# A two-layer hybrid encoder on one core: TensorE's order taken from a scheduler, or written out with delays in ticks

## The chip, the core and the metric

One core of a Trainium2 chip runs the whole program. The core has TensorE (PE, matrix products into PSUM), VectorE (DVE), ScalarE (ACT), GpSimd (POOL) and SyncE (SP), which issues most of the DMAs. The metric is the device time of one execution in microseconds (us); smaller is better. The median of three runs before the change is 1895.78 us (1894.39 to 1896.45).

## The reference

Sequence 512, model width 1024, two layers. Each layer normalizes x, projects it to 7168 columns, and mixes tokens in three ways: differential attention (4 heads, two softmaxes each over all 512 keys), a convolution module (gated linear unit, 31-tap depthwise convolution, layer norm, SiLU) and neighbourhood attention (8 heads, an 8 x 16 window on an 8 x 64 grid, with a bias). Sigmoid gates merge them. An FFN and a gated per-layer input ("ple") follow, and a last norm ends the program.

```python
for i in range(DEPTH):
    h = rmsnorm(x, norm_mix[i])
    qa, ka, va, glu_in, qc, kc, vc, gates = jnp.split(h @ w_in[i], SPLITS, axis=-1)
    ya = diff_attention(qa, ka, va, ...)
    yb = conformer_conv(glu_in, ...)
    yc = neighbourhood_attention(qc, kc, vc, rpb[i])
    ga, gb, gc = jnp.split(jax.nn.sigmoid(gates), 3, axis=-1)
    merged = ga * (ya @ w_br_a[i]) + gb * (yb @ w_br_b[i]) + gc * (yc @ w_br_c[i])
    x = x + merged @ w_o[i]
    h = rmsnorm(x, norm_ffn[i])
    x = x + (jax.nn.silu(h @ w_ffn_gate[i]) * (h @ w_ffn_up[i])) @ w_ffn_down[i]
    h = rmsnorm(x, norm_ple[i])
    x = x + jax.nn.sigmoid(h @ w_ple_gate[i]) * (p[i] @ w_ple_in[i])
return rmsnorm(x, norm_final)
```

## The kernel before

**Layout and products.** Activations lie transposed: a chunk is 128 model columns by 512 tokens, and h is 8 such chunks. Every operand is split into a high part (rounded to the format that PE multiplies) and a low part, the remainder; `mm3` (L116) makes three products for one: high x high, high x low, low x high. `gemm` (L122) sums up to eight chunks of rows into one PSUM tile of 128 x 512, 24 products of 512 columns. `weights` (L105) loads one block of 128 x 1024 with a DMA on SP's queue and splits it on ACT (high, L82) and DVE (low, L96), with a priority 400 instructions ahead of its place; there are two raw buffers and three split ones. PSUM has four tiles for projections (`mm`), two for scores (`sc`), one for transposes (`tr`) and one for value products (`av`).

**Who sets the order.** A scheduler orders each engine's instructions when the program is traced: among the ready ones it takes the earliest by program order, with weights moved ahead, going by a model of the durations. On the chip each engine then runs its own list in order. PE's order is set in this way too, so projections that come later in the program are put where attention waits.

**Norms.** The scale 1/rms is not applied to h but to each projection when it leaves PSUM (`self.rb`, one value per token, spread over partitions). `rows_rstd` (L136) makes it: four transposes of the sum of squares (L142), a reduce (L144) and a scalar step (L146) on DVE, the power -0.5 on POOL (L148), four transposes that spread it (L151). The instructions that need it come behind it in the program.

**One layer** (`layer`, L263): `glu` (8 projections), then four pairs of neighbourhood heads (`natten_in`, `natten_out`) and four heads of differential attention (`diff_in`, `diff_out`), each with its query and key projections, value products for every second one (`values`, L382, 256 columns wide), then `gate_c`, `branch_c`, `merge_a`, `gate_b`, `merge_b`, `w_o`, `ffn`, `ple`. `stack` (L566) brings queries and keys into their final place with four DMAs for a query and eight for a key on SP's queue; `rope` adds four more. A neighbourhood pair makes four units (two halves of the tokens, two heads): scores (L591), bias and softmax on DVE, ACT and POOL, transposes by PE (L476 to L481), a split out of PSUM, value products (L498 to L501). A head of differential attention does the same with two softmaxes (`probs`, L657; transposes L633, value products L639), and ends with a norm of its own over 128 columns.

**Convolution.** `taps` (L324) yields the 124 tap instructions of a layer, each on DVE over 128 x 512. `background` (L339) puts some of them behind given evictions, by the tuple `BG`: 4 behind each neighbourhood eviction, 2 behind each rope, 4 in gate C, 1 in branch C, 3 and 1 in merge A. `conv` (L351), called between merge A and gate B (AT = 8), sums the four tiles, has PE make the mean (L361), and normalizes.

**Start and end.** `build` loads the eight chunks of x in turn, with the first weight block in four pieces and the second whole, and PE starts on two blocks. `final` (L761) sums the squares, makes the power, transposes the result and stores it in eight DMAs of 256 KB.

Of the kernel before, what the change touches and what calls it, by code (L numbers as in the profile page):

```python
# [47 lines left out]
TUNE = {}  # L48
AT = 8
LOOK = 0  # L50
NORM = (1, 1)
START = (0, 1)
BG = (4, 2, 4, 1, 3, 4, 1, 4)
GAP = 464
# [7 lines left out]
class Net:  # L62
    def __init__(self, nc, tc, a):
        self.nc, self.tc, self.a = nc, tc, a
        self.uid = 0
        self.phase = "pre"
        self.act_set = None
        self.act_now = []
        self.act_prev = []

# [34 lines left out]
    def weights(self, ap, n, ahead=None, parts=1):  # L105
        with self.tc.high_priority(offset=self.w_ahead if ahead is None else ahead):
            raw = self.sb("wr", [P, 1024])
            hi = self.sb("wh", [P, 1024], F32R)
            lo = self.sb("wl", [P, 1024], F32R)
            for c in range(parts):  # L110
                s = slice(c * n // parts, (c + 1) * n // parts)
                self.nc.sync.dma_start(raw[:, s], ap[:, s])
                self.split(hi[:, s], lo[:, s], raw[:, s])
        return hi, lo
# [7 lines left out]
    def gemm(self, out, ap, acts, first=True, last=True):  # L122

        n = len(acts)
        for o in range(0, n, 8):
            c = min(8, n - o)
            wh, wl = (self.first.pop(0) if self.first
                  else self.weights(ap[:, o * P:(o + c) * P], c * P))
            for k in range(c):
                s = slice(k * P, (k + 1) * P)  # L130
                h = acts[o + k]
                h = h if isinstance(h, tuple) else (h[:, 0, :], h[:, 1, :])
                self.mm3(out, wh[:, s], wl[:, s], h[0], h[1],
                         first and o + k == 0, last and o + k == n - 1)

    def rows_rstd(self, sq, n):  # L136


        nc = self.nc
        st = self.ps("tr", (P, 4, P))  # L140
# [7 lines left out]
        nc.gpsimd.tensor_tensor(col, ms, self.power, ALU.pow)  # L148
        bc = self.ps("tr", (P, 4, P))
        for c in range(4):  # L150
            nc.tensor.transpose(bc[:, c, :], col[:, c:c + 1].to_broadcast([P, P]), self.ident)  # L151
        return col, bc.rearrange("p a b -> p (a b)")
# [6 lines left out]
    def norm_chunk(self, k, x, g, tag, st):  # L159
# [4 lines left out]
        self.sumsq(k, x, st)  # L164
# [11 lines left out]
    def build(self):  # L176
        nc, tc, a = self.nc, self.tc, self.a
        self.w_ahead = 400
        self.bufs = dict(wr=2, wh=3, wl=3, h=8, qk=4, kh=2, v=4, pt=2, y=5, z=5, x=8, t=8, rp=4,
                         e=4, a=3, r=4, ss=1, sm=8, rc=4, b=3, s=4)  # L180
        self.pbufs = dict(mm=4, sc=2, tr=1, av=1)
        tune = dict(TUNE)
        BG, AT, NORM, START, LOOK = (tune.pop(k, globals()[k]) for k in ("BG", "AT", "NORM", "START", "LOOK"))
        self.bg, self.at, self.norm, self.start, self.look = BG, AT, NORM, START, LOOK
        self.w_ahead = tune.pop("w_ahead", self.w_ahead)
        for t, n in tune.items():
            (self.pbufs if t in self.pbufs else self.bufs)[t] = n
        with tc.tile_pool(name="sb", bufs=1) as self.pool, \
# [3 lines left out]
            xsrc = a["xT"]  # L192
            h, st = [], []
            self.first = []
            self.parts = self.sb("par", [P, PAR], bufs=1)
            self.small()
            nc.sync.dma_start(self.parts, a["par"])
            self.consts()
            for k in range(KD):
                x = self.sb("x", [P, 512])  # L200
                nc.sync.dma_start(x, xsrc[k])
                h.append(self.norm_chunk(k, x, self.par(0, "mix", k), "h", st))
                if k in self.start:
                    m = len(self.first)
                    col0 = OFF_GLU + (CB if m % 2 == 0 else 0) + m // 2 * P
                    self.first.append(self.weights(a["w_in"][0, col0 // P], 1024, 0,
                                                   4 if m == 0 else 1))
            col, bc = self.rows_rstd(st[0], D)
            for i in range(L):
                h, col, bc = self.layer(i, h, col, bc, xsrc, xs)  # L210
                xsrc = xs
# [51 lines left out]
    def layer(self, i, h, col, bc, xsrc, xs):  # L263
        self.i, self.h = i, h
        self.col, self.rb = col, self.spread(bc)
# [5 lines left out]
        yc, ya, st, sd = [], [], {}, {}  # L271
        work = [(self.natten_in, self.natten_out, n, yc, st) for n in range(HC // 2)]
        work += [(self.diff_in, self.diff_out, n, ya, sd) for n in range(HA)]
        ready = []
        for n in range(len(work) + self.look):
            if n < len(work):
                w = work[n]
                ready.append(w[0](w[2], w[4]))
            if n >= self.look:
                w = work[n - self.look]  # L280
                w[1](w[2], w[3], *ready[n - self.look])
        acc = self.gate_c()
        self.branch_c(acc, yc)
        yb = []
        then = lambda m: yb.extend(self.conv(cs)) if m == self.at else None
        self.merge_a(ya, acc, then)
        gb = self.gate_b(then)
        then(2 * KD)
        mg = self.merge_b(yb, acc, gb)
        x, h, bc = self.w_o(mg, xsrc)  # L290
        self.rb = self.spread(bc)
        pairs = self.inputs()
        h, col, bc = self.ffn(h, x)
        self.rb = self.spread(bc)
        return self.ple(h, x, xs, pairs)

    def proj(self, col0):
        ps = self.ps("mm")
# [3 lines left out]
    def glu(self, zs):  # L302
        self.phase = "glu"
        nc = self.nc
        for j in range(4):
            pg = self.proj(OFF_GLU + CB + j * P)
            sg = self.sb("t", [P, 512])
            self.tt(sg, pg, self.rb, ALU.mult)
            self.act(sg, sg, AF.Sigmoid, table="sigmoid")
            pa = self.proj(OFF_GLU + j * P)  # L310
            ta = self.sb("t", [P, 512])
            self.tt(ta, pa, self.rb, ALU.mult)
            z = self.sb("z", [P, GW + 2 * HALO, GR])
            mid = z[:, HALO:HALO + GW, :]
            zc = self.tt(mid.rearrange("p a b -> p (a b)"), ta, sg, ALU.mult)
            nc.vector.memset(z[:, 0:HALO, 0:1], 0.0)
            nc.vector.memset(z[:, HALO + GW:, GR - 1:GR], 0.0)
            nc.vector.tensor_copy(z[:, 0:HALO, 1:GR], z[:, GW:GW + HALO, 0:GR - 1])
            nc.vector.tensor_copy(z[:, HALO + GW:, 0:GR - 1], z[:, HALO:2 * HALO, 1:GR])
            zs.append(z)  # L320
            if j:
                self.background(zc, self.bg[5])
# [28 lines left out]
    def conv(self, cs):  # L351
# [7 lines left out]
        self.tt(sm, sm, cs[3], ALU.add)  # L359
        mu = self.ps("tr")  # L360
# [5 lines left out]
        _, bc = self.rows_rstd(st[0], CB)  # L366
        rb = self.spread(bc)
        ys = []
        for j, c in enumerate(cs):
            self.tt(c, c, rb, ALU.mult)  # L370
            sg = self.sb("t", [P, 512])
            self.act(sg, c, AF.Sigmoid, table="sigmoid",
                     scale=self.par(i, "lg", j), bias=self.par(i, "lb", j))
            self.nc.vector.tensor_scalar(c, c, self.par(i, "lg", j), self.par(i, "lb", j),
                                         ALU.mult, ALU.add)
            y = self.sb("y", [P, 2, 512], F32R)
            self.tt(c, c, sg, ALU.mult)
            self.split(y[:, 0, :], y[:, 1, :], c)
            ys.append(y)
        return ys  # L380

    def values(self, ap):  # L382
# [7 lines left out]
        for o in range(0, KD, 4):  # L390
            wh, wl = self.weights(ap[:, o * 256:(o + 4) * 256], 1024)
            for k in range(o, o + 4):
                s = slice((k - o) * 256, (k - o + 1) * 256)
                for t in range(4):
# [5 lines left out]
                       stop=k == KD - 1 and t % 2 == 1)  # L400
        vs = []
# [11 lines left out]
    def natten_in(self, pr, st):  # L413

        self.phase = "natten"
        nc, i = self.nc, self.i
        if pr == 0:
            st["r8"] = self.sb("r", [P, 512])
            self.act(st["r8"], self.rb, AF.Copy, scale=0.125)
        if pr % 2 == 0:  # L420
            vs = self.values(self.a["w_vc"][i, pr // 2])


            edge = [vs[1][0:64, 0], vs[0][64:128, 1]]
            vd = [self.sb(tag, [P, 2, 256], F32R) for tag in ("ss", "x")]
            for n in range(2):
                for o in range(0, P, 64):
                    for part, v in enumerate(vd):
                        nc.sync.dma_start(v[o:o + 64, n].bitcast(F32), edge[n][:, part].bitcast(F32))
            st["v"] = vs, vd  # L430
        qk = []
        for off, r in ((OFF_QC, st["r8"]), (OFF_KC, self.rb)):
            ps = self.proj(off + pr * P)
            t = self.sb("t", [P, 512])
            self.background(self.tt(t, ps, r, ALU.mult), self.bg[0])
            qk.append(self.stack(t, off == OFF_KC))
        return (*qk, *st["v"])

    def natten_out(self, pr, ys, q, k, vs, vd):
        mm = self.nc.tensor.matmul  # L440
        self.phase = "natten"
        nc, i = self.nc, self.i
        y = self.sb("y", [P, 2, 512], F32R)
        ys.append(y)
        for half in range(2):
            av = self.ps("av", (P, 2, 256))
            for u in range(2):
                head = 2 * pr + u
# [446 lines left out]
```

## Time and profile before

| what | us |
|---|---|
| median of the runs | 1895.78 |
| the profiled execution, its own time | 1898.36 |
| its span, first to last instruction | 1896.6 |
| gated linear unit, layer 0, 28.4 to 57.3 | 28.9 (PE busy 28.9) |
| from there to the middle of attention, 57.3 to 146.3 | 89.0 (PE busy 88.33, DVE 70.49, ACT 48.94) |
| 146.3 to 249.2 | 102.9 (PE 101.67, DVE 78.43, ACT 64.88) |
| branch C, 328.6 to 352.2 | 23.6 (PE 22.49, DVE 21.99) |
| gate B, 417.5 to 463.6 | 46.1 (PE 45.50, DVE 28.27) |
| FFN, layer 0, 536.3 to 896.0 | 359.7 (PE 359.22, DVE 160.34) |

Windows are stretches of the span, in us from its start; layer 1 repeats layer 0 from 956 on. An engine's busy time is the union of its instructions. The products of PE overlap in the records (each is shown from its start to its modelled end), so PE's busy time says when PE is idle and not how fast it goes; the distance from one start to the next says that. The granted clock is the share of PE's clock that the chip let through; the profile has no record of it before 15.7 us.

### The profile page before, as it was taken

Reading aid. Unit: us, or ns where it says so; the run is one execution under the profiler, and the core shown is the slowest. Engines: PE = TensorE matmul, PEld = TensorE weight load, DVE = VectorE, ACT = ScalarE, POOL = GpSimd, SP = SyncE. Lnnn points to the kernel's source line nnn. Section 1 sums busy time; section 2 is a strip of 40 time slices with the busy share of each in tenths; the row PEclk is TensorE's granted clock in tenths of the full one; section 3 lists DMA queues with packets and bytes.
Section 4 is the critical chain, followed back from the end, with each engine's and each line's share of the span. In section 5 each row is a group of like instructions: output and inputs, shape, how many; then the busy total and the mean of one; then the engine's idle time right before and its main releaser. Section 6 shows DMA issues by size and latency. Waiting matters only on the chain.

```text
span 1896.6 us, 23617 instructions
## 1 busy us (share of the span) xinstructions
PE 1855.3 (98%) x8868; PEld 1536.8 (81%) x8868; DVE 1188.2 (63%) x1912; ACT 767.9 (40%) x1288; POOL 28.9 (2%) x87
## 2 busy tenths in 40 slices
PE   8999998999999999999999999899999999999998
PEld 6888877888888888888888888678888888888876
DVE  6787788975744434445767868799765444344454
ACT  4367564333432222333425656443434322222343
POOL 0000000000000000000000000000000000000000
PEclk9999998999999999999999999899999999999999
DMA  5555532332432233222436544413333222322222
GB/s 178 152 158 147 159 114 58 104 106 78 157 111 91 88 99 109 91 87 89 142 117 176 165 137 127 125 54 100 101 119 128 97 99 78 113 100 93 88 86 90
DMA packets 89795, 213.81 MB, mean 113 GB/s; under 512 B 12240, under 2 KB 29264, under 8 KB 89680
## 3 DMA queue, kind: packets, MB, share of 16 engines
q1 hardware_dynamic: 89680, 212.29, 35.5%
q8 instruction: 70, 1.15, 0.2%
q14 instruction: 45, 0.37, 0.1%
HBM read 176.59 MB, written 4.19 MB: 95 GB/s over the span
## 4 chain that ended last, share of the span: by engine, by line
PE 88%; DVE 4%; ACT 3%; DMA 2%; issue 1%; POOL 1%; SPq 0%; DVEq 0%; POOLq 0%; ACTq 0%
PE ffn_mm L118 13%; PE ffn_mm L120 13%; PE ffn_mm L119 13%; PE mergea_mm L118 2%; PE mergea_mm L120 2%; PE mergea_mm L119 2%; PE ple_mm L118 2%; PE ple_mm L119 2%; PE ple_mm L120 2%; PE diff_sc L591 2%; PE glu_mm L118 1%; PE wo_mm L119 1%; PE glu_mm L120 1%; PE wo_mm L120 1%; PE wo_mm L118 1%
## 5 line engine op out<-in xcount | busy, mean ns | idle before, releaser
L82 ACT ACTIVATE ffn_wh<-ffn_wr 128x1024 fp32r<-128x1024 f32 (+1 forms) x152 | 144.2, 949 | 513.0 <-issue 366.8
L119 PE MATMUL ffn_mm<-wo_h,ffn_wh 128*128 128x512 f32 x704 | 274.1, 389 | 0.0
L118 PE MATMUL ffn_mm<-wo_h,ffn_wh 128*128 128x512 f32 x704 | 274.0, 389 | 0.0
L120 PE MATMUL ffn_mm<-wo_h,ffn_wl 128*128 128x512 f32 x704 | 273.9, 389 | 0.0
L96 DVE TENSOR_TENSOR ffn_wl<-ffn_wr,ffn_wh 128x1024 fp32r<-128x1024 f32 (+1 forms) x152 | 164.8, 1084 | 123.6 <-ACT ffn_wh L82 123.6
L99 DVE SCALAR_TENSOR_TENSOR conv_z<-glu_z,pre_par,conv_z 128x512 f32<-128x512 f32 x240 | 178.8, 745 | 1.5
L120 PEld LDWEIGHTS ffn_mm<-wo_h,ffn_wl 128*128 128x128 f32 x704 | 132.2, 188 | 27.5
L119 PEld LDWEIGHTS ffn_mm<-wo_h,ffn_wh 128*128 128x128 f32 x704 | 132.2, 188 | 27.4
L118 PEld LDWEIGHTS ffn_mm<-wo_h,ffn_wh 128*128 128x128 f32 x704 | 132.2, 188 | 27.2
L96 DVE TENSOR_TENSOR ffn_t<-ffn_t,ffn_mm 128x512 f32<-128x512 f32 x44 | 30.2, 687 | 119.0 <-PE ffn_mm L120 119.0
L96 DVE TENSOR_TENSOR ffn_t<-ffn_mm,wo_r 128x512 f32<-128x512 f32 x44 | 30.4, 691 | 114.6 <-PE ffn_mm L120 114.6
L119 PE MATMUL ffn_mm<-ffn_y,ffn_wh 128*128 128x512 f32 x160 | 62.2, 389 | 0.0
L118 PE MATMUL ffn_mm<-ffn_z,ffn_wh 128*128 128x512 f32 x160 | 62.2, 389 | 0.0
L118 PE MATMUL ffn_mm<-ffn_y,ffn_wh 128*128 128x512 f32 x160 | 62.2, 389 | 0.0
L120 PE MATMUL ffn_mm<-ffn_y,ffn_wl 128*128 128x512 f32 x160 | 62.2, 389 | 0.0
L119 PE MATMUL ffn_mm<-ffn_z,ffn_wh 128*128 128x512 f32 x160 | 62.2, 389 | 0.0
L120 PE MATMUL ffn_mm<-ffn_z,ffn_wl 128*128 128x512 f32 x160 | 62.2, 389 | 0.0
L82 ACT ACTIVATE mergea_wh<-mergea_wr 128x1024 fp32r<-128x1024 f32 (+1 forms) x32 | 27.1, 846 | 79.5 <-PE mergea_mm L119 71.9
L666 DVE TENSOR_REDUCE diff_s<-diff_sc 128x1 f32<-128x512 f32 x64 | 43.7, 685 | 18.7 <-PE diff_sc L591 18.2
L82 ACT ACTIVATE natten_wh<-natten_wr 128x1024 fp32r<-128x1024 f32 x24 | 25.4, 1059 | 49.4 <-PE glu_mm L119 23.3
L96 DVE TENSOR_TENSOR wo_x<-wo_x,ffn_mm 128x512 f32<-128x512 f32 x32 | 22.0, 687 | 34.2 <-PE ffn_mm L120 34.2
L82 ACT ACTIVATE ple_wh<-ple_wr 128x1024 fp32r<-128x1024 f32 (+1 forms) x32 | 23.5, 734 | 41.3 <-issue 34.9
(429 smaller groups left out, 4735.3 us busy)
## 6 DMA issues: line engine op xcount, KB each, us to landing
ffn_wr<-w_fg SPq DMA_DIRECT2D x44, 512.0 KB, 3.2
ffn_wr<-w_fu SPq DMA_DIRECT2D x44, 512.0 KB, 3.2
ffn_wr<-w_fd SPq DMA_DIRECT2D x32, 512.0 KB, 3.5
natten_b<-bias SPq DMA_DIRECT2D x64, 128.0 KB, 2.2
natten_wr<-w_in SPq DMA_DIRECT2D x16, 512.0 KB, 3.4
diff_wr<-w_in SPq DMA_DIRECT2D x16, 512.0 KB, 3.8
gatec_wr<-w_in SPq DMA_DIRECT2D x16, 512.0 KB, 3.6
mergea_wr<-w_in SPq DMA_DIRECT2D x16, 512.0 KB, 3.2
```

What stands on the lines that cost most here:

```text
L82: i = self.nc.scalar.activation(out, in_, func, **kw)
L96: return self.nc.vector.tensor_tensor(out, a, b, op)
L99: return self.nc.vector.scalar_tensor_tensor(out, a, s, b, op0, op1)
L118: mm(out, wh, ah, start=first, stop=False)
L119: mm(out, wh, al, start=False, stop=False)
L120: mm(out, wl, ah, start=False, stop=last)
L591: self.nc.tensor.matmul(out, q[u][:, qs], st[u][:, ks], start=n == 0, stop=n == 1)
L666: nc.vector.tensor_reduce(out=m[:, u:u + 1], in_=sc, op=ALU.max, axis=AX.X, negate=True)
```

## The change

PE's instructions are no longer ordered by the scheduler: the body stands in `manual_schedule(engines={PE})`, and PE runs them as the program lists them. The other engines are ordered as before. To put work of attention, norms and convolution between projections, these parts become generators. `gemm` calls `chunk()` after each chunk of rows (three products), `values` twice for each of its chunks of twelve half-width products; four chunks make a tick. A generator yields the number of ticks after which its next part is listed, and `run` takes a delay for the first part.

```diff
+    def run(self, gen, delay=0):
+        e = [self.now + delay, gen, self.phase]
+        self.live.append(e)
+        if not delay:
+            self.step(e)
+        return e
...
+    def tick(self):
+        self.now += 1
+        for e in list(self.live):
+            while e in self.live and e[0] <= self.now:
+                self.step(e)
...
+    def chunk(self):
+        self.chunks += 1
+        if self.chunks % 4 == 0:
+            self.tick()
+
+    def ready(self, fn):
+        if self.rb is not None:
+            fn()
+        else:
+            self.wait.append((self.phase, fn))
...
-    def rows_rstd(self, sq, n):
+    def norm(self, sq, n, waits, done, spread=True):
...
+        yield waits[0]
         st = self.ps("tr", (P, 4, P))
...
         nc.gpsimd.tensor_tensor(col, ms, self.power, ALU.pow)
+        yield waits[1]
         bc = self.ps("tr", (P, 4, P))
...
+    def main_norm(self, sq, waits=(2, 2)):
+        self.col = self.rb = None
+        self.run(self.norm(sq, D, waits, self.rows))
```

While a norm is under way `self.rb` is None, and `ready` holds back the evictions that need it; `rows` releases them. For the last chunk of a norm the square is now made ahead of the operand. The numbers of buffers change: PSUM `mm` 4 to 3 and `tr` 1 to 2; SBUF `b` 3 to 4 and `s` 4 to 8.

The opening: the parameters and the first two chunks of x are loaded from ACT's queue, PE first makes 14 products on zeros, and then works on four weight blocks at once, chunk by chunk, each block loaded in pieces of 256, 256 and 512 columns into tiles of other tags.

```diff
+        nc.scalar.dma_start(self.parts, a["par"])
+        xc = [self.sb("x", [P, 512]) for _ in range(KD)]
+        for k in range(2):
+            nc.scalar.dma_start(xc[k], a["xT"][k])
+        self.consts()
+        warm = self.ps("av")
+        for _ in range(WARM):
+            nc.tensor.matmul(warm, self.zero_r, self.zero_r[:, None, :].to_broadcast([P, 4, P]),
+                             start=True, stop=True)
...
+        for k in range(KD):
+            if k > 1:
+                nc.sync.dma_start(xc[k], a["xT"][k])
+            pieces = {0: (0, 256, "t"), 2: (256, 512, "rp"), 4: (512, 1024, "e")}
...
+            for src, wh, wl, ps in blocks:
+                self.mm3(ps, wh[:, s], wl[:, s], h[k][:, 0, :], h[k][:, 1, :],
+                         k == 0, k == KD - 1)
...
+            if k == KD - 1:
+                self.sumsq(k, xc[k], st)
+                self.main_norm(st[0], (1, 1))
+            self.tick()
```

The layer: projections are listed ahead of the units that use them. `natten_in` now only projects and starts its four units, `natten_v` makes values for two pairs; `diff_in` and `diff_v` do the same for heads; `gate_c` makes one block at a call.

```diff
+        self.natten_in(0, sn, yc)
+        self.natten_v(0, sn)
+        self.natten_in(1, sn, yc)
+        self.natten_in(2, sn, yc)
+        self.natten_v(1, sn)
+        self.natten_in(3, sn, yc)
+        acc = []
+        self.diff_in(0, sd, ya)
+        self.diff_v(0, sd)
+        self.diff_in(1, sd, ya)
+        self.gate_c(acc, 0)
+        self.diff_in(2, sd, ya)
+        self.diff_v(1, sd)
+        self.diff_in(3, sd, ya)
+        for m in range(1, KD):
+            self.gate_c(acc, m)
...
+        for n in range(4):
+            self.run(self.natten_unit(pr, n // 2, n % 2, *qk, st, box, ys[pr]), 3 + n)
...
+        for qt in range(4):
+            self.run(self.diff_unit(head, qt, q, k, st, box, ys), 4 + 2 * qt)
```

A neighbourhood unit lists its scores and softmax, after 2 ticks its transposes and splits, after 1 more its value products. A unit of differential attention lists `probs` for one quarter of the tokens; every second one goes on after 2 ticks with the transposes of both, after 1 more with the value products, and at the end of a head with the head's norm, waits (1, 2). The tiles that hold the shifted values move from tag `ss` to `x`.

The convolution runs as a generator that starts before the second block of gate B and is driven to its end behind gate B; its taps are placed by `BG = dict(glu=4, natten=3, gatec=2, branchc=2, mergea=4, mergea2=3)`, that is 12, 24, 16, 16, 32 and 24 of them, none behind rope.

```diff
+            if m == 1:
+                conv = self.run(self.conv(cs, ys))
...
+        yield 2
         mu = self.ps("tr")
         nc.tensor.matmul(mu, self.ones, sm, start=True, stop=True)
...
+        yield from self.norm(st[0], CB, (3, 2), done)
```

The end: in the last layer the last chunk of `ple` is made in two halves of 256 tokens, with the sums of squares of the first half, its power and its transposes listed between the products of the second, and the result is stored in four DMAs of 512 KB. The small product of `ple` goes to a tile of tag `sc`.

```diff
+        pg = [self.ps("mm", (P, 256)), None]
+        products(pg[0], wg, h, 0, range(4))
+        total(0, most, range(4))
...
+        rest(pi[0], 0)
+        lows = [turn("av", 0, 0), turn("tr", 0, 1)]
+        pg[1] = self.ps("mm", (P, 256))
+        products(pg[1], wg, h, 1, range(6))
+        total(1, sq, (0, 1))
+        col = column(0)
+        products(pg[1], wg, h, 1, range(6, 8))
+        gate(pg[1], 1)
...
+        rest(pi[1], 1)
+        for c in range(2):
+            store(c, col[:, c:c + 1], (lows[c], turn("mm", 1, c)))
+        lows = [turn("sc", 0, 2), turn("sc", 0, 3)]
+        total(1, sq, (2, 3))
+        col = column(1)
+        highs = [turn(t, 1, 2 + c) for c, t in enumerate(("mm", "av"))]
+        for c in range(2):
+            store(2 + c, col[:, c:c + 1], (lows[c], highs[c]))
```

644 lines of the change are left out of this document (353 added, 291 removed).

## The prediction

> **What bounds the kernel now.** I read the page's busy times first, then the windows by stage, then TensorE's (PE's) waits, then its timeline around the longest ones. The profiled execution took 1898.36 us, 1896.6 of it span; the three timed runs have a median of 1895.78, 0.8 under the span. The sum below is made against the span and 0.8 is taken off at the end.
>
> ```profile
> PE 1855.3 (98%) x8868; PEld 1536.8 (81%) x8868; DVE 1188.2 (63%) x1912; ACT 767.9 (40%) x1288; POOL 28.9 (2%) x87
> ```
>
> PE is the bound, but 98% is not its peak: a 512-wide product is shown as 0.39 us busy and the next one starts 0.227 us later. So I count spacing. In the timeline undisturbed products start every 0.227 us (512 wide) and every 0.118 us (256 wide), and transposes every 0.109 us. Taking each of the 8868 spacings against these, 72 us are left over between the first product (5.63) and the last PE instruction. This excess is all that a better order can win inside. It lies in the opening (8), in two stretches at half clock (17), in waits at full clock (some 26) and in small change-over losses of under 0.25 us each (some 20), which any order has. FFN, gate B, merge B and merge A have almost none.
>
> ```profile
> 0.00:5.60 5.60, 0.00 (x0) 0.00 (x0) 1.68 (x9) 3.03 (x5) 1.24 (x9) 1.00 0.70 166
> 249.20:328.60 79.40, 73.07 (x347) 57.57 (x346) 65.76 (x113) 41.35 (x80) 2.57 (x5) 0.91 0.31 87
> 285.30:299.00 13.70, 10.71 (x35) 8.21 (x36) 8.96 (x16) 3.00 (x5) 1.01 (x1) 0.50 0.55 133
> 1220.60:1234.30 13.70, 10.71 (x36) 8.29 (x35) 9.24 (x17) 3.00 (x5) 1.01 (x1) 0.50 0.49 127
> 352.20:417.50 65.30, 65.30 (x290) 54.08 (x289) 53.85 (x76) 18.97 (x26) 0.00 (x0) 1.00 0.30 101
> ```
>
> Columns: window, us, busy time of PE, weight loads, VectorE (DVE), ScalarE (ACT), POOL, then granted clock, DMA share, GB/s. The second row is the end of differential attention: PE has holes there, and in the third and fourth the clock is 0.50. The last row is merge A: PE full, DVE 53.85 of 65.3 busy. It matters later.
>
> ```profile
> PE diff_tr L151 <- POOL diff_rc L148: 5.0, 6, 1.1
> PE diff_av L118 <- ACT diff_pt L82: 4.0, 6, 0.7
> PE diff_tr L633 <- DVE diff_a L99: 3.2, 2, 1.6
> PE diff_tr L142 <- ACT diff_ss L82: 2.5, 2, 1.3
> PE ffn_tr L151 <- POOL ffn_rc L148: 2.0, 2, 1.1
> PE wo_tr L151 <- POOL wo_rc L148: 1.5, 2, 0.8
> PE conv_tr L151 <- POOL conv_rc L148: 1.3, 2, 0.7
> ```
>
> Each norm makes PE wait for POOL's power between two sets of transposes (L151); a head's transposes and value products (L633, L118, L142) come before their inputs. In order of time, just before the clock drops:
>
> ```profile
> 283.35 0.27 PE L633 MATMUL diff_tr<-pre_ident,diff_a 128*128 128x128 f32 x1
> 285.23 0.82 PE L633 MATMUL diff_tr<-pre_ident,diff_a 128*128 128x128 f32 x3 [1.61 <-DVE diff_a L99]
> 293.93 1.11 PE L142 MATMUL diff_tr<-pre_ident,diff_ss 128*128 128x128 f32 x4 [1.26 <-ACT diff_ss L82]
> ```
>
> **The change part by part.** PE runs in the order in which the program is written; the other engines are still ordered as before. A tick is four chunks of 128 rows, 12 products: 12 x 0.227 = 2.72 us (value products: 24 x 0.118 = 2.83). What depends on other engines is put a fixed number of ticks later.
>
> *Norms.* Transposes come 1 or 2 ticks after the last square, the broadcast 1 or 2 after them. The chain between is one reduce (0.69), a scalar step (0.16) and the power (1.01, once 1.37), with hand-overs some 2.2 us: under one tick. The waits at L151 go: 5.0 + 2.0 + 1.5 + 1.3 and 0.9 for the ple norm, 10.7. Evictions that need the norm are held back; three PSUM buffers instead of four then carry 2 + 2 + 2 ticks, and the first is free about 1.5 us after tick 4, before the fourth product group needs it. Without that cover it would cost what it costs now. I take 10.7 (8 to 11).
>
> *Attention.* Scores, transposes and value products of a unit stand 2 and 1 ticks apart; eviction of a transposed tile (ACT 0.60, DVE 0.69) fits in a tick. The excess of the two half-clock stretches is 17.0 (idle 5.4 of it). The other waits at full clock on attention's and W_o's rows sum to 13.1 - 5.4 = 7.7. I take both, 24.7; ends 0 (the dips and waits come back) and 24.7.
> [...]
>
> *New waits.* (1) The first neighbourhood unit stands 3 ticks after its key projection: 3 x 2.83 + 0.45 for the clearing products, 8.9 us. In the trace the same chain, from the eviction at 80.38 over ACT, DVE and SyncE's copies to the landing at 88.84, takes 8.5 plus 0.3 of hand-over. Level; behind it stand the value projections. I charge 1 us a layer (0 to 2.5). Later pairs have other units inside their ticks, so more room; a rope chain (13 us) has 4 ticks plus units, 14 or more.
> (2) Convolution taps: 40 of them leave attention and gate C for branch C and merge A. Merge A had 32 and gets 8 x 7 = 56. Four taps in a row took 3.10, 0.78 each where one waits for the other, 0.66 else; so DVE has 53.85 + 24 x 0.66 to 0.78, 69.7 to 72.7 us of work in 65.3 of PE's: it ends 4.4 to 7.4 late. What is late next is the mean's product, 10.9 us (four ticks) into gate B; before it DVE must do the lag, two weight splits (2 x 1.14), one eviction (0.6) and three sums (3 x 0.69): 9.4 to 12.4. I take 1.5 a layer (0 to 4).
> (3) 32 units a layer, 64, in fixed order: any that comes late holds the projections behind it. Attention's waits now are 13.1 / 64 = 0.2 each; I take 0.08, 5 us (0 to 13). Together 2 + 3 + 5 = 10.
>
> *SyncE and POOL.* The stack copies, bias tiles and memsets are the same in number; each stack copy keeps SyncE 0.6 us, 12 per pair, 7.2 of some 20 us of PE time. Free.
>
> *Opening.* Now: first product at 5.63, excess 8.2 until 28.4, lost 13.8. New: 14 products on zeros from about 1.6 us (their tile is written by 1.52) at the half-clock spacing of 0.427 end at 7.6; then four blocks run chunk by chunk, 96 products, 21.8 us. They need 4.3 MB; at the 250 GB/s at which 2.7 MB came by 12.9 us, the last chunk lands near 19, before PE needs it at 26.7. Loss 7.6, gain 6.2. But the next two weight blocks (1.05 MB) have a priority 400 instructions ahead and free buffers, so SyncE may issue them first: 4.2 us later, gain 2. If the clock also came as late as now (full at 15.7, 10.1 us after the first product), -3. I take 5.
> [...] No run here shows products on zeros.
>
> *Last norm.* From the last ple product (1883.08) to the end are 13.5 us: two sums, squares, the power (1887.29 to 1888.30), eight stores issued in 4.05 us. With the chunk in halves the first 1 MB leaves while the second half is made; the second chain has half-width steps (0.42 for 0.69), then two stores. I estimate 10.5: gain 3 (0 to 5). Thirty 512-wide products as sixty at 0.118 cost 0.3 of it.
>
> Sum: 10.7 + 24.7 + 5 + 3 - 10 = 33.4. Span 1863.2, time **1862**. With every new wait at zero, 1852; with the opening and the end at their best too, 1849; less some of the change-over losses, 1840.
>
> **The rivals.**
> *The clock dip stays* (0.14): PE still idles beside transposes near the last heads, now behind gate C. For: it takes only a few us of holes. Against: each unit now has projections before and behind it. Costs the 17 again: 1879.
> *VectorE becomes the bound* (0.12): DVE does 290.5 us of work in the 360 between 57.3 and 417.5; without the holes there are some 330. If the lag reaches evictions, and the convolution's chain holds PE 6 us a layer instead of 1.5, and 3 more at its norm, 15: 1877.
> *The fixed order holds PE* (0.12, slower): a static order cannot slip past a late unit as the old one did at 270 to 280, where gate C's products fill in. Place: the scores and transposes of the 64 units. If each waits as the longest L151 waits do, 1.1 us, 70 instead of 5: 1927. It decides from (33.4 + 5) / 64 = 0.6 us a unit. For: the copies' and bias tiles' landings (2 to 5 us) vary. Against: the distances are over the measured chains. [...]
> *It does not do what it says* (0.04): ACT, DVE and SyncE, still ordered by priority, shift the same waits elsewhere: 1896.
> *Better* (0.08): under 1848, nearly all waits gone.
>
> **How the numbers follow.** The forecast's own case (0.50) covers 1848 to 1872. Faster by over 0.2% (3.8 us, about what a measurement of this kernel can tell): 0.50 + 0.14 + 0.12 + 0.08 = 0.84; same 0.04; slower 0.12. The range leaves out the slower case and most of what is under 1840: 1838 to 1897.
>
> **What would show it.** L151's waits gone from PE's list; clock 1.00 through attention; first real product at 7.6 to 10, at 0.227 spacing; taps at the head of DVE's lag at merge A's end, and a wait of PE at the mean's product of 0 to 4 us; no list of natten_sc, natten_tr or diff_sc waits over 10 us in sum. Wrong if PE's waits on units sum to over 38 us, or if the half clock remains.

## The result and the profile after

The changed kernel takes 1900.84 us (median, 1899.12 to 1901.63) beside 1895.68 us of the kernel before on the same chip (1894.22 to 1896.77): a ratio of 1.0026, 95% interval 1.0015 to 1.0037. It is slower by a quarter of a per cent. I had forecast 1862.

The profiled execution took 1901.63 us, 1899.8 of it span. First the busy times on its page, then PE's longest waits (in all, times, longest), then windows by stage (us, then busy time of PE, weight loads, VectorE, ScalarE, POOL, then granted clock, DMA share, GB/s): attention with gate C and branch C, then merge A, then gate B.

```profile
PE 1850.4 (97%) x8912; PEld 1551.0 (82%) x8912; DVE 1190.5 (63%) x1921; ACT 769.3 (40%) x1296; POOL 29.3 (2%) x88
```

```profile
PE conv_tr L465 <- DVE conv_ss L139: 6.7, 2, 3.4
PE diff_tr L750 <- DVE diff_sm L186: 5.0, 2, 2.5
PE diff_sc L702 <- DMA diff_x<-diff_rp: 4.3, 2, 2.3
PE diff_sc L702 <- DMA diff_qk<-diff_kh: 4.3, 6, 1.4
PE diff_tr L750 <- DVE diff_a L142: 3.4, 4, 1.3
PE diff_sc L702 <- ACT diff_a L125: 3.2, 2, 1.6
PE pre_mm L159 <- ACT pre_y L125: 2.9, 2, 2.5
PE ple_tr L926 <- DVE ple_ss L139: 2.2, 1, 2.2
```

```profile
56.40:351.00 294.60, 279.83 (x1593) 242.56 (x1592) 218.39 (x439) 163.05 (x343) 9.40 (x34) 0.98 0.46 131
351.00:416.30 65.30, 65.30 (x289) 54.08 (x289) 64.55 (x93) 19.03 (x25) 0.00 (x0) 1.00 0.31 101
416.30:466.90 50.60, 47.24 (x203) 38.29 (x202) 36.62 (x54) 19.80 (x28) 1.01 (x1) 0.97 0.22 73
```

No wait for POOL's power is left (the old L151). New names stand at the top: the convolution's mean, the head's norm, the scores' inputs. Nearly every one comes twice, once a layer, at the same place: an order that is written out repeats its waits. Attention's stretch is as long as before (294.6 for 294.9) and still at clock 0.98; gate B has grown.

The two spans by stretch, with what my terms say of each (their sum is the 33.4 on record) and, in the last column, the best version found below:

| stretch | before | after | forecast | measured | best |
|---|---|---|---|---|---|
| start to the first neighbourhood projection | 57.3 | 56.4 | -5.0 | -0.9 | -5.5 |
| attention to branch C, both layers | 589.7 | 588.6 | -22.7 | -1.1 | -38.3 |
| merge A and gate B, both layers | 222.9 | 231.8 | +1.7 | +8.9 | -1.3 |
| merge B of layer 0 to attention of layer 1 | 528.8 | 525.7 | -2.7 | -3.1 | -3.2 |
| merge B of layer 1 to the end | 497.9 | 497.3 | -4.7 | -0.6 | -3.7 |
| sum | 1896.6 | 1899.8 | -33.4 | +3.2 | -52.0 |

**Where PE waits, and what follows a wait.** The timeline of PE around the scores of head 1 in layer 0 (start, us, operation, in brackets the idle time before it and what ended it), and SyncE's queue ahead of it:

```profile
215.81 0.47 PE L702 MATMUL diff_sc<-diff_x,diff_qk 128*128 128x512 f32 x1 [2.04 <-DMA diff_x<-diff_rp]
217.63 0.77 PE L702 MATMUL diff_sc<-diff_qk,diff_qk 128*128 128x512 f32 x1 [1.36 <-DMA diff_qk<-diff_kh]
```

```profile
200.12 1.14 SPq L710 DMA_DIRECT2D diff_rp<-diff_rp  x2
202.76 1.14 SPq L695 DMA_DIRECT2D diff_qk<-diff_kh  x2
203.99 1.19 SPq L696 DMA_DIRECT2D diff_qk<-diff_rp  x2
205.22 1.22 SPq L710 DMA_DIRECT2D diff_rp<-diff_rp  x2
...
212.09 1.15 SPq L695 DMA_DIRECT2D diff_x<-diff_kh  x2
```

The key leaves PSUM at 199.26. Two of its four rotating copies (L710) are issued, then four copies of the query's stack, which waited for their data, and only then the other two: 6.3 us for four copies that take 2.4. The key's stack is issued from 212.09 on, and the second product of the first score group starts at 217.63, 18.4 us after the key left PSUM. PE stood there at 213.77, 14.5 us after it.

Windows around three such waits, the wait first and what follows it behind:

```profile
213.20:216.60 3.40, 1.03 (x7) 0.52 (x5) 3.40 (x6) 1.80 (x4) 0.00 (x0) 1.00 0.86 201
216.60:223.40 6.80, 5.62 (x13) 4.00 (x14) 3.89 (x8) 2.28 (x5) 0.00 (x0) 0.50 0.59 169
247.30:250.70 3.40, 1.51 (x5) 0.97 (x6) 3.14 (x7) 2.63 (x8) 0.00 (x0) 1.00 0.62 169
250.70:254.10 3.40, 3.40 (x9) 2.62 (x8) 2.83 (x8) 2.49 (x7) 0.00 (x0) 0.51 0.14 52
428.20:431.60 3.40, 0.87 (x3) 0.49 (x3) 2.38 (x3) 0.65 (x2) 0.00 (x0) 1.00 0.18 51
431.60:435.00 3.40, 3.40 (x9) 2.68 (x8) 3.08 (x5) 2.37 (x4) 0.00 (x0) 0.51 0.27 104
```

Each of these places, with some 2 us or more of waiting in it, is followed by 3.41 or 6.83 us at half clock, and the windows of 3.4 us at half clock above have 9 products where 15 fit at the full clock's spacing of 0.227. Per layer there are four such places, 17.07 us at half clock; before there was one of 13.65. By my estimate, half of the stretch behind it, such a wait costs its length and then up to 1.7 or 3.4 us more. It does not always: no half clock follows the 2.47 us that PE waits in the opening of this trace, before 9.10 (the clock is 1.00 from 4.98 to 216.61; the last section counts when one followed).

### The profile page after: what moved, and what is told of

Its sections match the earlier page's. It is cut to its first block, busy times and chain, and to the rows that moved or that the text cites. A ratio compares the mean times of both kernels' runs of the same rounds, so it can differ in the third digit from the quotient of the medians.

```text
span 1899.8 us, 23913 instructions
## 1 busy us (share of the span) xinstructions
PE 1850.4 (97%) x8912; PEld 1551.0 (82%) x8912; DVE 1190.5 (63%) x1921; ACT 769.3 (40%) x1296; POOL 29.3 (2%) x88
## 4 chain that ended last, share of the span: by engine, by line
PE 87%; DVE 6%; DMA 3%; ACT 2%; SPq 1%; issue 1%; DVEq 0%; POOL 0%; POOLq 0%; ACTq 0%
PE ffn_mm L161 13%; PE ffn_mm L159 13%; PE ffn_mm L160 13%; PE mergea_mm L160 2%; PE mergea_mm L159 2%; PE mergea_mm L161 2%; PE wo_mm L159 2%; PE wo_mm L161 2%; PE wo_mm L160 2%; PE ple_mm L159 2%; PE ple_mm L160 2%; PE ple_mm L161 1%; PE natten_mm L159 1%; PE natten_mm L161 1%; PE natten_mm L160 1%; PE diff_mm L160 1%
## 5 line engine op out<-in xcount | busy, mean ns | idle before, releaser
L125 ACT ACTIVATE natten_e<-natten_b,natten_s 128x256 f32<-128x256 f32 x64 | 32.2, 503 | 27.1 <-DVE natten_s L565 25.8
```

The costliest lines, as they stand in the source:

```text
L125: i = self.nc.scalar.activation(out, in_, func, **kw)
```

## The experiments

The theory: PE's order is good, but at four places per layer, in the opening and at the end it stands one or two ticks too early, and the half clock adds to each. The rivals: the fixed order as such is worse and waits only move; or VectorE has become the bound.

**The rope chain.** Differential units two ticks later.

```diff
-            self.run(self.diff_unit(head, qt, q, k, st, box, ys), 4 + 2 * qt)
+            self.run(self.diff_unit(head, qt, q, k, st, box, ys), 6 + 2 * qt)
```

> The units of differential attention start 6 ticks behind their key projection instead of 4. Theory of the late chain: in the changed kernel the key's copies of rope stand on SyncE's queue behind the query's stack copies, the chain takes some 19 us and is over the distance; the scores' waits for copies (4.3 + 4.3 us on PE's list) and the half-clock stretch of 6.8 us that follows in each layer (3.4 us lost in each) go: 13 to 15 us less, 1886 to 1888. Rival, the waits only move: the units of two heads meet other steps and VectorE is as late as before, 1898 to 1904.

Measured 1879.66 us, ratio 0.9909 (0.9896 to 0.9923), against 1.0026 of the changed kernel: 22 us, more than expected. PE's waits now:

```profile
PE conv_tr L465 <- DVE conv_ss L139: 7.6, 2, 3.8
PE diff_tr L750 <- DVE diff_a L142: 4.6, 8, 0.7
PE diff_sc L702 <- ACT diff_a L125: 2.3, 2, 1.2
```

Both DMA waits of the scores are gone, and the head norm's wait with them (5.0 to 0.7). In the changed kernel the norm's transposes (L184) fell on the tick of the next half's transposes (L750), which then wait for the norm's reduce:

```profile
266.28 0.60 PE L184 MATMUL diff_tr<-pre_ident,diff_ss 128*128 128x128 f32 x4
266.71 0.60 PE L750 MATMUL diff_tr<-pre_ident,diff_a 128*128 128x128 f32 x4
269.82 0.66 PE L750 MATMUL diff_tr<-pre_ident,diff_a 128*128 128x128 f32 x4 [2.51 <-DVE diff_sm L186]
```

Of six half-clock stretches in the two layers' attention one is left; the one behind the mean grew from 3.41 to 6.83 us in both layers. This one delay brings 22 of the 39 us between forecast and result, but it removes two kinds of wait at once, so the 22 are not the rope chain's alone. The chain itself is hardly shorter: from a key's eviction to the last landing it takes 17.5 to 21.9 us here, 19.5 to 22.4 in the changed kernel. Only the room grew.

**The head norm alone.** First wait of the norm of a head 2 ticks instead of 1.

```diff
-        yield from self.norm(sq, P, (1, 2), done, spread=False)
+        yield from self.norm(sq, P, (2, 2), done, spread=False)
```

> A head's norm puts its first transposes 2 ticks behind the value products instead of 1. Theory of the collision: with a wait of 1 they fall on the tick of the next head's transposes, three tiles are asked of the two transpose tiles, and PE waits for VectorE's reduce (5.0 us) and the next spread (1.7 us); these go, and the half-clock stretch of 3.4 us behind them in each layer: 8 to 10 us less, 1891 to 1893. Rival, VectorE is simply late there: the wait goes to the next transposes, 1898 to 1902.

Measured 1903.07 us, 1.0029 (1.0018 to 1.0041): a miss. The wait is gone, but others took its place:

```profile
PE diff_sc L702 <- DMA diff_qk<-diff_kh: 14.9, 10, 5.1
PE diff_sc L702 <- DMA diff_x<-diff_rp: 6.4, 3, 2.3
```

With the 2.1 us at 286.33 below, the scores wait 23.4 us for the keys' copies instead of 8.6. The rival has the time nearly right (1898 to 1902) and the place wrong: the wait went to the scores and not to the next transposes. The new ones stand at head 3, once a layer:

```profile
273.28 3.49 SPq L710 DMA_DIRECT2D diff_rp<-diff_rp  x4
286.33 0.47 PE L702 MATMUL diff_sc<-diff_x,diff_qk 128*128 128x512 f32 x1 [2.09 <-DMA diff_x<-diff_kh]
291.34 0.77 PE L702 MATMUL diff_sc<-diff_qk,diff_qk 128*128 128x512 f32 x1 [4.54 <-DMA diff_qk<-diff_kh]
```

All four rotating copies of this key now stand behind the query's stack copies on SyncE's queue, from 273.28 on; in the changed kernel two of them were issued ahead of these, at 267.81. And nothing holds PE at the norm any more, so it comes to the scores earlier. Without room for the rope chain a longer distance in one place moves the wait.

**The convolution, in two ways.** First the mean two ticks later, then fewer taps in merge A with the mean where it was.

```diff
-        yield 2
+        yield 4
         mu = self.ps("tr")
```

> The convolution's mean is listed 4 ticks behind its start in gate B instead of 2. Theory of a fixed distance too short for VectorE's lag of taps: the wait at the mean (6.7 us in both layers) and the half-clock stretch of 3.4 us behind it go: 8 to 10 us less, 1891 to 1893. Rival, VectorE is the bound of this stretch: its lag comes out at the convolution's norm or at merge B, 1898 to 1902.

Measured 1891.54 us, 0.9969 (0.9957 to 0.9980), 11 us less than the changed kernel, where 8 to 10 were expected; conv_tr is gone from the list.

```diff
-BG = dict(glu=4, natten=3, gatec=2, branchc=2, mergea=4, mergea2=3)
+BG = dict(glu=4, natten=4, gatec=4, branchc=2, mergea=3, mergea2=1)
```

> The changed kernel, with one edit: 17 or so of the convolution's taps per layer go from merge A back into attention and gate C (per eviction 4 for neighbourhood, 4 in gate C, 1 in the second half of merge A). Theory (the mean's product waits because VectorE is behind with its taps in merge A): conv_tr's wait for conv_ss (6.7 us) and the half-clock windows beside it go; gate B falls from 50.6 to some 46 us per layer, 8 to 10 us in all, about 1891; attention's VectorE gets fuller and may give 0 to 5 of it back. Rival (the mean stands too early whatever VectorE has to do): gate B stays at 50, 1899 to 1905.

Measured 1887.54 us, 0.9955 (0.9942 to 0.9967), 13 us less, more than expected; merge A and gate B:

```profile
349.30:414.60 65.30, 65.30 (x290) 54.07 (x289) 54.99 (x79) 19.08 (x25) 0.00 (x0) 1.00 0.32 101
414.60:460.00 45.40, 45.40 (x204) 37.20 (x203) 31.10 (x46) 19.82 (x29) 1.01 (x1) 1.00 0.26 81
```

VectorE has 55.0 us of work in merge A instead of 64.6 and comes out without a lag; gate B takes 45.4 instead of 50.6. Both edits remove the same loss, so the cause is VectorE's lag against a fixed place of the mean. Attention and gate C, with some 22 taps more (147 DVE instructions from merge A through gate B became 125), did not get longer. The half clock differs in other places too, though the waits there are as they were: the first trace lacks the window near 250, the second lacks one of the two near 217 and the one near 1200, and both have one in the opening, near 9, that the changed kernel's trace has not. Each is worth up to 1.7 us by the same estimate, so the two gains are the mean's only to within a few us.

**The opening.** The weights' priority of 400 instructions is switched off until tick 10.

```diff
-        with self.tc.high_priority(offset=self.w_ahead):
+        with self.tc.high_priority(offset=0 if self.now < 10 else self.w_ahead):
```

> Until the tenth tick weight blocks are loaded and split in program order, not 400 instructions ahead. Theory: the two blocks of later projections, which now lead SyncE's queue and ScalarE's list, delay the first real product to 9.05 us; it comes at 7 to 8, PE's wait for the first operand (2.5 us) goes, 1.5 to 3 us less, 1898 to 1899.5. Rival: the opening is bound by what the DMA engines bring in all, and the next block is then late itself: 1900 to 1903.

Measured 1896.73 us, 0.9999 (0.9990 to 1.0008): 5 us less than the changed kernel, more than expected. PE and ACT in the changed kernel:

```profile
4.96 1.06 ACT L125 ACTIVATE glu_wh<-glu_wr 128x1024 fp32r<-128x1024 f32 x1 [1.33 <-DMA glu_wr<-w_in]
...
7.71 1.04 ACT L125 ACTIVATE glu_wh<-glu_wr 128x1024 fp32r<-128x1024 f32 x1
8.65 1.32 ACT L125 ACTIVATE pre_y<-glu_t 128x256 fp32r<-128x256 f32 x4
```

```profile
5.54 1.09 PE L269 MATMUL pre_av<-pre_zeror 128*128 128x512 f32 x4
9.10 0.50 PE L159 MATMUL pre_mm<-glu_h,pre_y 128*128 128x512 f32 x1 [2.47 <-ACT pre_y L125]
```

ACT splits two blocks of 128 x 1024 that nobody needs before 34 us ahead of the four pieces that PE waits for. In program order the first real product follows the zeros without a gap:

```profile
5.50 1.09 PE L269 MATMUL pre_av<-pre_zeror 128*128 128x512 f32 x4
6.60 0.49 PE L159 MATMUL pre_mm<-glu_h,pre_y 128*128 128x512 f32 x1
```

**Together.** The three edits (delay 6, mean 4, weights in order):

> Rope units 2 ticks later, the convolution's mean 2 ticks later and the opening's weights in program order, together. Theory (three separate losses in three places): the parts add, 0.0117 + 0.0057 + 0.0027 of the time before off 1.0026, ratio 0.9825, about 1863 us; PE's waits for diff_qk and diff_x by DMA and for conv_ss are gone at once, and of the half-clock windows at most one per layer is left, in attention. Rival (the waits only move, as with the longer waits of the head norm alone): ratio above 0.988, and waits of over 1.5 us appear in new places.

Measured 1865.53 us, 0.9836 (0.9823 to 0.9850), against 0.9825 for the sum: the parts add to within 2 us, so they are separate losses. Two half-clock windows are left in layer 0 (at 78.0 and 245.3) and none in layer 1; I had expected at most one a layer.

**Two units on one tick.** Around 246.5 the changed kernel puts two `probs` on one tick: four score groups for two tiles, of which the third and the fourth wait:

```profile
248.55 0.50 PE L702 MATMUL diff_sc<-diff_x,diff_qk 128*128 128x512 f32 x1 [1.61 <-ACT diff_a L125]
249.92 0.50 PE L702 MATMUL diff_sc<-diff_x,diff_qk 128*128 128x512 f32 x1 [0.64 <-ACT diff_e L125]
```

One block of gate C between heads 1 and 2 parts them.

```diff
         self.diff_in(1, sd, ya)
         self.gate_c(acc, 0)
+        self.gate_c(acc, 1)
         self.diff_in(2, sd, ya)
```

> As r5_three, and one more block of gate C stands between head 1's and head 2's projections, so that no two probability units of two heads fall on one tick. Theory (two units on one tick want four score groups from two score tiles): the waits of scores for diff_a and diff_e (some 3 us in all) go, and with them the 3.41 us window near 248: 3 to 6 us below r5_three in the two layers. Rival (the tiles are not the reason, the rows' softmax on ScalarE is just late): no gain, within 1.5 us of r5_three.

Measured 1860.49 us, 0.9811 (0.9798 to 0.9825), 5 us less; the waits of diff_sc for ACT are gone, and no half clock is left between 5 and 1841 us. Of the two windows that went, the one at 78.0 lies ahead of the edit, so up to 1.7 of the 5 us need not be its doing.

**Three more distances.** Neighbourhood units 4 ticks behind their key instead of 3, the head norm (2, 2), the last norm's first sums behind all of its products.

```diff
-            self.run(self.natten_unit(pr, n // 2, n % 2, *qk, st, box, ys[pr]), 3 + n)
+            self.run(self.natten_unit(pr, n // 2, n % 2, *qk, st, box, ys[pr]), 4 + n)
...
-        products(pg[0], wg, h, 0, range(4))
+        products(pg[0], wg, h, 0, range(8))
...
-        products(pg[0], wg, h, 0, range(4, 8))
```

> As r6_gap, and three waits that are left get one tick or more: the head norm's first wait 1 to 2 ticks, the neighbourhood units 3 to 4 ticks behind, the last norm's first half moved behind all eight of its products. Theory: natten_sc's wait for natten_qk by DMA (1 to 2 us), the head norm's transposes (0.7 us and what is left of them) and ple_tr's wait (2.2 us) go: 3 to 6 us below r6_gap. Rival (a longer norm only pushes the next head's key or unit, as it did without the longer rope): level with r6_gap or above.

Measured 1855.44 us, 0.9783 (0.9770 to 0.9797), 5 us less. Three of them come from the end (ple_tr's wait is 0.8 instead of 2.2, and the half clock behind it is gone). In attention natten_qk's wait went, but natten_s on VectorE rose from 1.9 to 5.8: half of that edit was wrong.

**The transposes' distance.** From r7_rest, transposes of a differential unit 3 ticks behind the scores instead of 2; then the neighbourhood units back at 3.

```diff
         if t == 0:
             return
-        yield 2
+        yield 3
```

> As r7_rest, with the transposes of a differential unit 3 ticks behind its scores instead of 2. Theory (VectorE's last step of the softmax is late by up to 2.4 us): diff_tr's waits for diff_a (7.0 us) go and 4 to 7 us with them, 1849 to 1852. Rival (the three tiles of diff_a are held a tick longer, so the scores' exponentials wait in their place): waits of diff_sc come back, 1854 to 1862.

> As r11_tr3, with the neighbourhood units 3 ticks behind their key again. Theory (with 4 ticks more of them fall together with others: natten_sc's wait for natten_s on VectorE went from 1.9 to 5.8 us): natten_s back to 1.9, natten_qk's landing back at 2.8, so level with r11_tr3 or 1 to 2 us below. Rival (natten_s waits came from the longer head norm): 2 to 3 us above it.

Measured 1849.85 us, 0.9757 (0.9743 to 0.9770), and 1846.85 us, 0.9741 (0.9728 to 0.9754). The first is as expected, the second 3 us below it where 1 to 2 were. The last is the best version: 2.6% under the kernel before, with as many PE, DVE, ACT and POOL instructions as the changed kernel. Its page and its longest waits:

```profile
PE 1827.2 (99%) x8912; PEld 1540.7 (84%) x8912; DVE 1189.5 (64%) x1921; ACT 766.2 (42%) x1296; POOL 28.7 (2%) x88
```

```profile
PE natten_sc L703 <- DMA natten_qk<-natten_kh: 2.7, 2, 1.5
PE diff_av L160 <- DVE diff_pt L139: 2.5, 4, 0.9
```

VectorE does the same 1190 us in a span 55 us shorter, so it was not the bound.

**Products on zeros.** One instead of 14, from r7_rest.

```diff
-WARM = 14
+WARM = 1
```

> As r7_rest, with 1 product on zeros instead of 14. Theory (any product lifts the clock, some 3.4 us after the first): the first real products run at half clock for 3 to 4 us, 1.5 to 2 us slower than r7_rest. Rival (the clock comes as late as in the kernel before, 10.1 us after the first product): 4 to 5 us slower. Second rival (PE waits for weights in the opening anyway): within 0.7 us.

Measured 1858.59 us, 0.9803 (0.9789 to 0.9816), 3 us more, between the theory and its rival. The first real product starts at 6.55 and the full clock comes at 9.70, 3.15 us later, as in the theory; the opening is 1.2 us longer (attention starts at 52.7 for 51.5). The rest I put down to two more half-clock windows in layer 0's attention, whose waits are the same as in r7_rest: the last section has what the traces show of that.

**Is it the idleness?** In the changed kernel two waits per layer are filled with products on zeros.

```diff
         mu = self.ps("tr")
+        for _ in range(13):
+            nc.tensor.matmul(mu, self.zero_r, self.zero_r[:, None, :].to_broadcast([P, 4, P]), start=True, stop=True)
...
             sc = self.ps("sc")
+            for _ in range(fill[u]):
+                nc.tensor.matmul(sc, self.zero_r, self.zero_r[:, None, :].to_broadcast([P, 4, P]), start=True, stop=True)
```

> The changed kernel, with two of its waits per layer filled by products on zeros that nothing reads: 13 of them (3.0 us at 0.227) ahead of the convolution's mean, 8 and 5 ahead of the two score groups of head 1's first unit. The waits for data stay as long as they were; only PE is busy during them. Theory (the half clock is set by PE's idleness in these waits): the windows of 6.83 us near 216.6 and of 3.41 us near 431.6 go in both layers, and with them half of their length, (6.83 + 3.41) / 2 = 5.1 per layer: about 10 us below the changed kernel, 1889 to 1894; the windows near 250.7 and 271.2, whose waits are not filled, stay. Rival (the windows come from the kind of work there, transposes and two-product score groups, or from something outside PE): the windows stay and the time is that of the changed kernel, 1897 to 1905.

In the profiled execution (1891.46 us) both stretches are at full clock in both layers; the wait itself is as long as it was. The windows at head 1 and at the mean:

```profile
212.30:215.70 3.40, 3.39 (x19) 2.31 (x17) 3.40 (x5) 2.52 (x4) 0.00 (x0) 1.00 0.62 144
215.70:219.10 3.40, 1.79 (x7) 1.31 (x8) 2.66 (x5) 0.09 (x1) 0.00 (x0) 1.00 0.93 201
219.10:222.50 3.40, 3.40 (x17) 2.79 (x16) 1.16 (x4) 2.19 (x5) 0.00 (x0) 1.00 0.59 198
427.30:430.70 3.40, 3.24 (x12) 2.37 (x13) 2.18 (x5) 1.35 (x3) 0.00 (x0) 1.00 0.47 154
430.70:434.10 3.40, 3.40 (x16) 2.82 (x15) 2.39 (x4) 1.24 (x3) 0.00 (x0) 1.00 0.00 0
```

But the median of its 11 runs is 1896.34 (1891.46 to 1899.92), 1.0002 (0.9993 to 1.0011): 4.5 us less than the changed kernel, not 10. The mean clock was 0.998 in the profiled run and 0.992 to 0.995 in the others (0.989 in the changed kernel's profile), so some windows came back there; which, no trace shows. Nor is the profiled execution's gain the filling's alone: of the four places in the two layers that were not filled, three are at full clock in it as well (the one near 267 is left), though I had expected them to stay. That the half clock follows PE's idleness in these traces is shown by the filled places (1.00 in the windows above, 0.50 at the same places of the changed kernel) and by the count in the last section; the price of each place in the median is open.

## Why the prediction was wrong

*The bound, and the norms: right.* PE's excess over its undisturbed spacing is what moved. The waits at L151 (10.7) are gone, and the stretch of layer 0's FFN and ple norms gained 3.1 where I had 2.7.

*The failed step: the new waits,* charged at 10. They came to some 37: 28 in attention, 6.7 at the mean, 2.2 at the end. Attention gained 1.1 instead of 22.7. The first of my three terms held (natten_qk waits 1.6 us, charged at 2); the second, the taps' 3, came to 6.7, and the third, the units' 5, to some 27. It is the third that failed.
- I took the rope chain as 13 us against 14 or more. The room was 14.5, but the chain took 18.4. At head 1 the query's four stack copies between the key's rotating copies are 3.9 us of it. That is not all: head 2's rotating copies are issued in a row, and its chain is as long (19.5 us from the eviction to the last landing, 19.6 at head 1). The shortest chain of the kernel before took 16.6 (1123.09 to 1139.71), so my 13 had no row behind it. I had counted the copies as free by their sum (7.2 of 20 us) and had not followed their order.
- I spread 5 us over 64 units. The loss sits in few places: head 1's key, two units on one tick, the norm's and the next half's transposes on one tick. A fixed order makes each of them again in every layer. I had not laid out which steps fall on the same tick, which the program alone would have shown.
- The taps' lag was the right mechanism with a size too small: 11 taps (some 8.2 us), not 4.4 to 7.4, were left at merge A's end (taps from branch C were late too: 60 ran from the start of merge A on, where 56 are listed), and PE waits 3.4 a layer, inside my 0 to 4 but above the 1.5 charged. Left out was what follows it: gate B lost 4.5 a layer, with the half clock behind the wait.

*The clock.* I had the two dips go with their waits, as they did in the best version (clock 1.00). That was assumed: no run before the change shows what ends a dip, and the 17.0 us that I took for the two rest on it. In the changed kernel the new waits brought their own: 27.3 us at half clock in attention, as much as the two dips had. So the sign that I had named for being wrong, that the half clock remains, came. What the traces show of it is in the last section. In the window before the first dip of the kernel before, PE was busy for 1.46 of 3.41 us:

```profile
281.94:285.35 3.41, 1.46 (x8) 1.03 (x9) 3.41 (x7) 2.06 (x3) 0.00 (x0) 1.00 0.04 10
```

*The opening.* I took 5, and named the case in which the next weights are issued first (gain 2). That case came, with a gain of 0.9; in program order the gain is 5.5, between the 5 taken and the 6.2 of my sum. My loss of 7.6 has the products behind the zeros at the full clock, which no run before the change shows. In the changed kernel the clock's record begins, at 1.00, while the zeros run: at 4.98, 3.4 us after the first of them at 1.57, and there their spacing falls from 0.427 to 0.23. In the other eleven traces with 14 zeros it begins 3.3 to 5.9 us after the first. The other case, the full clock 10.1 us after the first product, did not come.

*The last norm.* 3 forecast. A wait of 2.2 for its half sums and the half clock behind it (3.41 us from 1882.31) took the gain back; with the sums moved, the end is 3.1 shorter than in the changed kernel.

*The rivals.* What happened is the slower one, the fixed order holding PE, with its point at 0.6 us a unit: attention's 28 us of waits are 0.44 a unit, and the half clock behind them (27.3 us, worth up to 13.7) brings it to at most 0.66. Its form was wrong: not every unit late by 1.1 us, but three places a layer in attention, and a fourth at the mean, late by 2 us or more. The range's upper end, 1897, left it out. *The clock dip stays* had the size of the half clock right and its place wrong. VectorE as the bound fell.

## What to carry to other kernels

When an order is written out by hand, list for each step the chain that feeds it as the queues will really interleave it (copies of one tensor between those of another), and which steps fall on the same tick and want the same tiles; an average wait per unit hides the few places that recur in every layer. Move only one distance at a time and look where the wait goes: a longer distance helped where the chain behind it had room, and cost where it had not. In this program a TensorE wait of 2 us or more has to be priced with the half clock that can follow it (3.41 or 6.83 us in the changed kernel).

## What the runs showed of the hardware

In these traces the half clock goes by a fixed grid. Within a trace, every half-clock stretch begins at a whole multiple of 3.413 us from every other; in the changed kernel's first layer they begin at 216.61 and 10, 16 and 63 times 3.413 us later. I took PE's idle time in each window of that grid (time not covered by a product or transpose at its undisturbed spacing, 0.227, 0.118 or 0.109 us) over the 14 traces, from 30 to 1820 us, for windows at full clock with over 1.2 us of idle time and transposes together:

```
idle in the window   windows   next window at half clock
under 2.0 us             184       0
2.0 to 2.2 us              8       3
over 2.2 us               46      45
```

A few ns more or less in the spacings move the 184 by a dozen or so and the other two rows not at all. So in these traces about 2.1 us of idle in one window were enough, and transposes count as work: windows with some 2.6 us of idle and transposes together (1.8 idle) kept the clock. Why one window with 2.6 us of idle kept it is open. A wait that lay across a border of the grid was split, and no half clock followed. In r7_rest natten_sc waits 2.47 us for natten_s in layer 0, on both sides of the border at 169.5, and the clock stays 1.00; it waits 0.45 + 2.03, the same sum, within one window in layer 1, and the next is at 0.50:

```profile
169.50:172.90 3.40, 1.68 (x14) 1.69 (x15) 2.66 (x12) 2.73 (x10) 0.00 (x0) 1.00 0.60 152
172.90:176.30 3.40, 3.40 (x30) 3.36 (x29) 1.18 (x3) 3.32 (x9) 0.00 (x0) 1.00 0.88 205
1084.30:1087.70 3.40, 0.97 (x6) 0.76 (x7) 3.34 (x11) 2.65 (x7) 0.00 (x0) 1.00 0.54 153
1087.70:1091.10 3.40, 3.40 (x19) 3.40 (x18) 1.02 (x7) 2.13 (x8) 0.00 (x0) 0.50 0.83 192
```

PE made 30 instructions in the window after the first and 19 after the second. From this I infer that an edit in one place can shift the grid under waits in another and change the time by some us. It fits the run with one product on zeros, where the wait at layer 0 now lies within one window; no run moved the grid alone, so it is not shown.
